# Up-projections of five FFNs, weights stationary and without transposes

## The chip, the cores and the metric

The kernel runs on one core of one Trainium2 chip. The metric is the device time of one execution in microseconds, the median of the runs. The engines are named as in the profile: PE is TensorE (PEld its weight loads), DVE VectorE, ACT ScalarE, POOL GpSimd, SP the queue that issues the DMAs.

## The reference

Two residual blocks over 256 tokens of 1024 channels, in fp32. What the change touches is the feed-forward network, which stands five times in the whole (two in each layer of the first block, one in the second block):

```python
def swiglu(x, w_in, w_out):
    gate, up = jnp.split(x @ w_in, 2, axis=-1)
    return (jax.nn.silu(gate) * up) @ w_out

x = x + 0.5 * swiglu(rms_norm(x, ffn1_norm_g[i]), ffn1_w_in[i], ffn1_w_out[i])
...
def swiglu_2(h, w_gate, w_up, w_down):
    return (jax.nn.silu(h @ w_gate) * (h @ w_up)) @ w_down
```

There are 2816 hidden channels, so `w_in` is 1024 x 5632 (the last FFN has gate and up as two matrices) and `w_out` 2816 x 1024. Between the FFNs stand the mixers: an mLSTM, a sliding-window attention, each with an attention over a memory, and a state-space mixer.

## The kernel before

Every product is made of fp32r parts: a weight is split into `whi` (rounded) and `wlo` (the rest), an activation into hi and lo, and three matmuls, hi x hi, hi x lo and lo x hi, are added up in PSUM.

**Weights.** A chunk is 128 x 1024 weights (512 KB), one step of the inner dimension K for 1024 columns, or two steps for 512. `plan` lists all chunks of the program in the order of use. `load` issues the DMA into one of 5 `raw` buffers, `prepare` (L316) casts `raw` to `whi` on ScalarE (L324) and subtracts on VectorE to make `wlo` (L325, by the helper at L122), each into one of 9 buffers. `need(c)` prepares up to 7 chunks ahead, but no more than 9 beyond the chunks used up.

**Token-major products**, `gemm` (L391): the stationary operand is the activation, 128 tokens by 128 of K, the moving one 512 columns of weights, and the result has tokens on the partitions (L418 hi x hi, L419 hi x lo of the weight, L420 lo x hi). **Channel-major products**, `gemm_ch` (L429), are used in some mixers: the stationary operand is 128 x 128 weights, the moving one the 256 tokens (L440 to L442), and the result has channels on the partitions.

**The FFN.** `ffn_in` takes the hidden channels in six blocks, five of 512 and one of 256. In a block gate and up of both token tiles grow in four PSUM banks (pool `mm`, four banks); ScalarE applies Silu (L563, L569), VectorE multiplies. The down-projection needs the result with channels on the partitions, so `operand_block` has TensorE transpose it (`split_t`, L453, four 128 x 128 to a bank of the other pool), ScalarE copies out the hi part (L455), VectorE the lo part. `residual_gemm` is the down-projection: token-major, the transposed hidden rows stationary (they are called `s` in the profile), added to the residual. `NormT` holds the normed and transposed input of an FFN or mixer, `xh` and `xl`.

**What sets the order.** The kernel is written with a tile library that orders the instructions of each engine by priority and places the waits; each engine then takes its instructions in that order. Transposes and side work are put in between the chunks by `defer`, `later` and `tick`.

Of the kernel before, what the change touches and what calls it, by code (L numbers as in the profile page):

```python
# [10 lines left out]
F32 = mybir.dt.float32  # L11
# [6 lines left out]
P = 128  # L18
# [44 lines left out]
class Operand:  # L63
    """A transposed activation, rows of K on the partitions, as an exact sum hi + lo."""
# [11 lines left out]
class Chunk:  # L76
    """One weight transfer of 1024 elements a partition and the products its columns take part in."""
# [8 lines left out]
def hybrid_kernel(ctx: ExitStack, tc: tile.TileContext, *aps, names=None):  # L86
# [7 lines left out]
    xtp = ctx.enter_context(tc.tile_pool(name="xtp", bufs=4))  # L94
# [46 lines left out]
    # ------------------------------------------------------------ constants  # L141
# [23 lines left out]
    # parameters by channel, transposed once  # L165
# [33 lines left out]
    # rows on every partition  # L199
# [3 lines left out]
    # ------------------------------------------------------------ weights  # L203
# [12 lines left out]
    def spec_ffn_in(w, w_up=None):  # L216
# [13 lines left out]
        blocks = []  # L230
        for b in range(5):
            blocks.append([add(pair(k, 1, 512 * b, 512 * b + 512), [(k, "g", 0, 512), (k, "u", 512, 512)])
                           for k in range(8)])
        blocks.append([add(pair(k, 2, 2560, 2816), [(k + i, "gu", i * 512, 512) for i in range(2)])
# [100 lines left out]
    # Work that the products hide: steps of generators and delayed calls, taken between the chunks.  # L335
# [38 lines left out]
    def pipeline(units, dist):  # L374
        """Starts a unit at each step; a unit goes on to its next stage every dist steps."""
# [15 lines left out]
    def gemm(chunks, xop, evac, groups=None, by_key=False):  # L391
        """Token-major products: evac(tok, key, psum) after each accumulation."""
# [36 lines left out]
    def gemm_ch(chunks, xop, evac):  # L429
        """Channel-major products of 512 columns: evac(pair, psum) with two tiles of 128 channels."""  # L430
# [17 lines left out]
    # ------------------------------------------------------------ activations  # L448
    def split_t(src, nk, dsts):
        """src [tokens, nk*128] transposed, as hi and lo in dsts (APs of [P, nk, 128])."""  # L450
# [15 lines left out]
    def direct_block(op, tok, k0, ps, nk):  # L466
        """An operand from a psum that already holds it transposed."""
# [7 lines left out]
    class NormT:  # L475
        """The normed residual, transposed, for products of either kind."""

        def __init__(self):
            self.filled = set()
            self.hi = [xtp.tile([P, 4, 2, P], F32R, tag="xt", name=nm("xh")) for _ in range(2)]  # L480
            self.lo = [xtp.tile([P, 4, 2, P], F32R, tag="xt", name=nm("xl")) for _ in range(2)]
# [4 lines left out]
        def stat(self, tok, kt):  # L486
            return self.hi[kt // 4][:, kt % 4, tok, :], self.lo[kt // 4][:, kt % 4, tok, :]

# [11 lines left out]
    def inv_rms(sums):  # L500
        """(sums[0] + sums[1] + EPS) ** -0.5 of two columns"""
# [8 lines left out]
    def normed(src, gains, put):  # L510
        """src(j) are the two halves of a row; put(j, normed half)"""
# [20 lines left out]
    def residual_gemm(chunks, xop, scale, after, tail=TAIL):  # L532
        """residual += scale * product; after(tok) when a tile is whole"""
# [15 lines left out]
    def norm_after(row, queue=nc.sync):  # L549
        """An operand to be filled by the gemm before, and the function that fills it."""  # L550
        dst = NormT()
        gains = gain_rows(row, queue)
        return dst, lambda t: norm_residual(t, gains, dst)

    def ffn_in(blocks, xop):
        h = Operand()
        for b, cs in enumerate(blocks):
            keep = {}

            def evac(t, key, ps, b=b, keep=keep):  # L560
                if key == "g":
                    keep[t] = slot()
                    act.activation(out=keep[t], in_=ps, func=AF.Silu)  # L563
                elif key == "u":
                    tt(keep[t], keep[t], ps, ALU.mult)
                    operand_block(h, t, 4 * b, keep[t], 4, D_FFN)
# [830 lines left out]
```

## Time and profile before

| | us |
|---|---|
| median of 3 runs (1619.86 to 1621.65) | 1620.25 |
| span of the profiled execution | 1618.5 |
| PE busy | 1599.2 (99%) |
| PEld busy | 1339.0 (83%) |
| DVE busy | 966.7 (60%) |
| ACT busy | 822.5 (51%) |
| DMA read | 280.34 MB, 174 GB/s over the span |

The profile shows one execution; apart from its span no time of that execution is given. Busy time of PE counts the whole length of a matmul, of which several are under way at once; how long one holds up the next is seen from the starts in the timeline alone. Shares are means over stages that differ.

### The profile page before, as it was taken

How to read it: one execution, taken by the hardware profiler on the slowest of the kernel's cores; microseconds unless marked ns; L12 is line 12 of the kernel's file. 1: busy time of each engine (PE TensorE's matmuls, PEld its weight loads, DVE VectorE, ACT ScalarE, POOL GpSimd, SP SyncE). 2: the span in 40 equal slices, each digit the busy share in tenths (PEclk: the TensorE clock that was granted, in tenths of full speed). 3: DMA queues.
4: the chain of work that ended last, by engine and by line, in shares of the span. 5: the costliest groups of instructions: out<-in, count | busy, mean ns of one | idle time of the engine just before them, and what ended most of it. 6: DMA issues, size and time to landing. Idle time of an engine off the chain costs nothing.

```text
span 1618.5 us, 21426 instructions
## 1 busy us (share of the span) xinstructions
PE 1599.2 (99%) x8124; PEld 1339.0 (83%) x8124; DVE 966.7 (60%) x1372; ACT 822.5 (51%) x1170; POOL 40.7 (3%) x72
## 2 busy tenths in 40 slices
PE   9999999999999999999999999999999999999998
PEld 7888898788888888888788888889899988888886
DVE  6555475558555555546765655368788864575552
ACT  6444365546444444444564544357856553454442
POOL 0000010100000000001100000000000000000000
PEclk9999999999999999999999999999999999999999
DMA  8665374446656566564333766565455566466560
GB/s 271 209 188 196 115 263 144 156 130 211 192 184 196 168 197 187 188 196 164 122 88 108 223 193 195 156 197 184 156 158 145 155 195 182 156 221 188 188 198 27
DMA packets 126971, 282.80 MB, mean 175 GB/s; under 512 B 12286, under 2 KB 23698, under 8 KB 126868
## 3 DMA queue, kind: packets, MB, share of 16 engines
q1 hardware_dynamic: 126868, 281.43, 55.0%
q8 instruction: 64, 1.05, 0.3%
q14 instruction: 39, 0.32, 0.1%
HBM read 280.34 MB, written 1.05 MB: 174 GB/s over the span
## 4 chain that ended last, share of the span: by engine, by line
PE 94%; DVE 2%; issue 1%; ACT 1%; DMA 1%; POOL 1%; SPq 0%; POOLq 0%; ACTq 0%; DVEq 0%
PE ps L418 25%; PE ps L420 25%; PE ps L419 25%; PE ps L440 3%; PE ps L441 3%; PE ps L442 3%; PE ps L453 3%; DMA raw<-in_ffn_w_in_dram 1%; PE ps L625 1%; PE ps L1010 1%; PE ps L1252 1%; POOL t L508 1%; PE ps L1032 1%; DVE wlo L122 1%; ACT whi L324 1%
## 5 line engine op out<-in xcount | busy, mean ns | idle before, releaser
L122 DVE TENSOR_TENSOR wlo<-raw,whi 128x1024 fp32r<-128x1024 f32 (+1 forms) x521 | 628.5, 1213 | 440.3 <-ACT whi L324 433.8
L324 ACT CAST whi<-raw 128x1024 fp32r<-128x1024 f32 (+1 forms) x521 | 543.0, 1044 | 556.4 <-PE ps L420 474.3
L418 PE MATMUL ps<-whi,xh 128*128 128x512 f32 (+2 forms) x1168 | 459.5, 394 | 3.0 <-DVE s L122 1.5
L420 PE MATMUL ps<-whi,xl 128*128 128x512 f32 (+2 forms) x1168 | 451.3, 387 | 0.3 <-DVE xl L122 0.2
L419 PE MATMUL ps<-wlo,xh 128*128 128x512 f32 (+2 forms) x1168 | 450.8, 386 | 0.0
L418 PE MATMUL ps<-whi,s 128*128 128x512 f32 x696 | 278.9, 401 | 0.3 <-ACT s L1329 0.3
L419 PE MATMUL ps<-wlo,s 128*128 128x512 f32 x696 | 274.5, 394 | 0.0
L420 PE MATMUL ps<-whi,s 128*128 128x512 f32 x696 | 274.1, 394 | 0.0
L418 PEld LDWEIGHTS ps<-whi,xh 128*128 128x128 f32 x1168 | 219.7, 188 | 48.1 <-DVE s L122 2.3
L420 PEld LDWEIGHTS ps<-whi,xl 128*128 128x128 f32 x1168 | 219.5, 188 | 45.9 <-DVE xl L122 0.9
L419 PEld LDWEIGHTS ps<-wlo,xh 128*128 128x128 f32 x1168 | 219.9, 188 | 41.5 <-issue 0.3
L420 PEld LDWEIGHTS ps<-whi,s 128*128 128x128 f32 x696 | 130.7, 188 | 30.7
L418 PEld LDWEIGHTS ps<-whi,s 128*128 128x128 f32 x696 | 130.8, 188 | 30.4 <-ACT s L1329 0.8
L419 PEld LDWEIGHTS ps<-wlo,s 128*128 128x128 f32 x696 | 130.9, 188 | 28.7
L440 PE MATMUL ps<-xh,whi 128*128 128x256 f32 x448 | 129.8, 290 | 0.0
L441 PE MATMUL ps<-xl,whi 128*128 128x256 f32 x448 | 127.6, 285 | 0.0
L442 PE MATMUL ps<-xh,wlo 128*128 128x256 f32 x448 | 127.6, 285 | 0.0
L440 PEld LDWEIGHTS ps<-xh,whi 128*128 128x128 f32 x448 | 86.4, 193 | 1.7 <-issue 0.2
L441 PEld LDWEIGHTS ps<-xl,whi 128*128 128x128 f32 x448 | 86.4, 193 | 0.4 <-issue 0.2
L442 PEld LDWEIGHTS ps<-xh,wlo 128*128 128x128 f32 x448 | 86.2, 193 | 0.1
L453 PE MATMUL ps<-ident,s 128*128 128x128 f32 x444 | 66.7, 274 | 2.0 <-DVE s L131 2.0
L453 PEld LDWEIGHTS ps<-ident,s 128*128 128x128 f32 x444 | 54.3, 141 | 16.4 <-issue 1.9
(211 smaller groups left out, 971.8 us busy)
## 6 DMA issues: line engine op xcount, KB each, us to landing
raw<-in_ffn_w_in_dram SPq DMA_DIRECT2D x160, 512.0 KB, 4.7
raw<-in_ffn_w_out_dram SPq DMA_DIRECT2D x88, 512.0 KB, 3.4
raw<-in_w_in_dram SPq DMA_DIRECT2D x80, 512.0 KB, 4.1
raw<-in_a_w_in_dram SPq DMA_DIRECT2D x24, 512.0 KB, 4.6
raw<-in_w_gate_dram SPq DMA_DIRECT2D x44, 256.0 KB, 3.1
raw<-in_w_up_dram SPq DMA_DIRECT2D x44, 256.0 KB
raw<-in_w_down_dram SPq DMA_DIRECT2D x22, 512.0 KB, 3.4
raw<-in_ffn_w_in_dram SPq DMA_DIRECT2D x32, 256.0 KB, 3.3
```

Of the source, the lines that this page charges most:

```text
L122: (eng or dve).tensor_tensor(out=o, in0=a, in1=b, op=op)
L324: act.copy(out=c.hi[:, 0:n], in_=c.raw[:, 0:n])
L418: pe.matmul(out=o, lhsT=xh, rhs=wh, start=first, stop=False)
L419: pe.matmul(out=o, lhsT=xh, rhs=wl, start=False, stop=False)
L420: pe.matmul(out=o, lhsT=xl, rhs=wh, start=False, stop=last)
L440: pe.matmul(out=o, lhsT=wh, rhs=xh, start=kt == 0 and j % 2 == 0, stop=False)
L441: pe.matmul(out=o, lhsT=wh, rhs=xl, start=False, stop=False)
L442: pe.matmul(out=o, lhsT=wl, rhs=xh, start=False, stop=kt == nk - 1 and j % 2 == 1)
L453: pe.transpose(out=ps[:, i * P:(i + 1) * P], in_=src[:, i * P:(i + 1) * P], identity=ident)
L508: pool_e.tensor_tensor(out=o, in0=a, in1=mhalf[:, 0:1].to_broadcast([P, n]), op=ALU.pow)
L625: pe.transpose(out=ps[:, i * P:(i + 1) * P], in_=src[:, i * P:(i + 1) * P], identity=ident)
L1010: pe.matmul(out=s[:, i * w:(i + 1) * w], lhsT=qt[half, (hh // 2) * P:(hh // 2 + 1) * P], rhs=bkt[half, g * SEQ:g * SEQ + w], start=True, s ...
```

## The change

In blocks 1 to 5 of each up-projection the roles are swapped. A half (gate or up of one block) is loaded as four chunks of two K steps by 512 columns, and `gemm_hidden` goes over its four tiles of 128 channels: for each K step the `whi` piece is stationary and meets 512 columns, the hi and the lo of the 256 tokens side by side, and then the `wlo` piece meets the 256 hi columns. The left half of the bank then holds hi x hi + lo x hi, the right half hi x lo, and the evacuation adds the two (ScalarE copies the right half, VectorE adds the left). Gate tiles get a Silu, up tiles a multiplication and a split into hi and lo, which are the operand of the down-projection as they are. `NormT` keeps hi and lo in one tile, so that both can be read as one row of 512. Block 0 stays token-major. The last block, 256 channels, has gate and up in the same four chunks, two tiles of each.

```diff
-    xtp = ctx.enter_context(tc.tile_pool(name="xtp", bufs=4))
+    xtp = ctx.enter_context(tc.tile_pool(name="xtp", bufs=2))
...
-        blocks = []
-        for b in range(5):
-            blocks.append([add(pair(k, 1, 512 * b, 512 * b + 512), [(k, "g", 0, 512), (k, "u", 512, 512)])
-                           for k in range(8)])
-        blocks.append([add(pair(k, 2, 2560, 2816), [(k + i, "gu", i * 512, 512) for i in range(2)])
+        def half(h, k, c0):
+            m = w if w_up is None else (w, w_up)[h]
+            src = m.rearrange("(k p) c -> p k c", p=P)
+            off = h * DFF if w_up is None else 0
+            return [(lambda raw: view(raw, 2, 512), src[:, k:k + 2, off + c0:off + c0 + 512])]
+        blocks = [[add(pair(k, 1, 0, 512), [(k, "g", 0, 512), (k, "u", 512, 512)]) for k in range(8)]]
+        for b in range(1, 5):
+            blocks.append([[add(half(h, k, 512 * b), [(k + i, 0, i * 512, 512) for i in range(2)])
+                            for k in range(0, 8, 2)] for h in range(2)])
+        blocks.append([add(pair(k, 2, 2560, 2816), [(k + i, 0, i * 512, 512) for i in range(2)])
                        for k in range(0, 8, 2)])
...
-            self.hi = [xtp.tile([P, 4, 2, P], F32R, tag="xt", name=nm("xh")) for _ in range(2)]
-            self.lo = [xtp.tile([P, 4, 2, P], F32R, tag="xt", name=nm("xl")) for _ in range(2)]
+            self.x = [xtp.tile([P, 4, 2, 2, P], F32R, tag="xt", name=nm("xt")) for _ in range(2)]
+            self.hi = [x[:, :, 0] for x in self.x]
+            self.lo = [x[:, :, 1] for x in self.x]
...
+        def both(self, kt):
+            return self.x[kt // 4][:, kt % 4].rearrange("p h a b -> p (h a b)")
...
+    def gemm_hidden(chunks, xop, tiles, evac):
+        for i in range(tiles):
+            ps = bank(mm)
+            for c in chunks:
+                if i == 0:
+                    need(c)
+                for kt, _, off, _ in c.entries:
+                    sl = slice(off + i * P, off + (i + 1) * P)
+                    pe.matmul(out=ps, lhsT=c.hi[:, sl], rhs=xop.both(kt), start=kt == 0, stop=False)
+                    pe.matmul(out=ps[:, 0:SEQ], lhsT=c.lo[:, sl], rhs=xop.mov(kt)[0], start=False, stop=kt == 7)
+                if i == tiles - 1:
+                    used[0] += 1
+                if c is chunks[1] or c is chunks[3]:
+                    tick()
+            evac(i, ps)
...
+        def both_parts(dst, ps):
+            act.copy(out=dst, in_=ps[:, SEQ:2 * SEQ])
+            tt(dst, ps[:, 0:SEQ], dst, ALU.add)
+
+        for b in range(1, 6):
+            gate = [slot() for _ in range(2 if b < 5 else 1)]
+            up = [slot() for _ in gate]
+            hi, lo = [[slot(F32R) for _ in gate] for _ in range(2)]
+
+            def gate_evac(i, ps, gate=gate):
+                both_parts(half(gate, i), ps)
+                act.activation(out=half(gate, i), in_=half(gate, i), func=AF.Silu)
+
+            def up_evac(i, ps, b=b, gate=gate, up=up, hi=hi, lo=lo):
+                u, a, z = half(up, i), half(hi, i), half(lo, i)
+                both_parts(u, ps)
+                tt(u, u, half(gate, i), ALU.mult)
+                act.copy(out=a, in_=u)
+                tt(z, u, a.bitcast(F32), ALU.subtract)
+                for t in range(2):
+                    h.parts[t, 4 * b + i] = (a[:, t * P:(t + 1) * P], z[:, t * P:(t + 1) * P])
+            if b < 5:
+                gemm_hidden(blocks[b][0], xop, 4, gate_evac)
+                gemm_hidden(blocks[b][1], xop, 4, up_evac)
+            else:
+                gemm_hidden(blocks[b], xop, 4, lambda i, ps: gate_evac(i, ps) if i < 2 else up_evac(i - 2, ps))
```

The order on TensorE near the start of block 2 of the first FFN, before (`ps` are banks, `s` the product of Silu and up that is transposed, `xh` and `xl` the input):

```order
L418 MATMUL ps_121_609<-whi_89_433,xh_2_113 128x512
L419 MATMUL ps_121_609<-wlo_90_434,xh_2_113 128x512
L420 MATMUL ps_121_609<-whi_89_433,xl_4_115 128x512
L453 MATMUL ps_124_615<-ident_79,s_113_576 128x128 x4
L418 MATMUL ps_118_597<-whi_95_460,xh_2_113 128x512
L419 MATMUL ps_118_597<-wlo_96_461,xh_2_113 128x512
L420 MATMUL ps_118_597<-whi_95_460,xl_4_115 128x512
L418 MATMUL ps_119_601<-whi_95_460,xh_2_113 128x512
L419 MATMUL ps_119_601<-wlo_96_461,xh_2_113 128x512
L420 MATMUL ps_119_601<-whi_95_460,xl_4_115 128x512
L453 MATMUL ps_130_636<-ident_79,s_114_585 128x128 x4
```

And in the same FFN with the change, the first and last pair of block 1's first tile, and the first pair of its second (`xt` holds hi and lo of the input; what is left out repeats the pair by K steps):

```order
L574 MATMUL ps_69_379<-xt_2_113,whi_50_246 128x512
L575 MATMUL ps_69_379<-xt_2_113,wlo_51_247 128x256
...
L574 MATMUL ps_69_379<-xt_3_114,whi_77_394 128x512
L575 MATMUL ps_69_379<-xt_3_114,wlo_78_395 128x256
L574 MATMUL ps_94_447<-xt_2_113,whi_50_246 128x512
L575 MATMUL ps_94_447<-xt_2_113,wlo_51_247 128x256
```

A bank is filled by 16 matmuls in a row and then left, where before four banks took turns by chunks; the transposes of these blocks are gone.

On VectorE, the last up tiles of block 3 with the change (`s_159`, `s_160` are up tiles, `s_157`, `s_158` gate, `s_163`, `s_164` the lo parts; a `wlo` row prepares a chunk of a later half):

```order
L122 TENSOR_TENSOR s_159_873<-ps_194_1030,s_159_873 128x256
L122 TENSOR_TENSOR s_159_873<-s_159_873,s_157_871 128x256
L122 TENSOR_TENSOR s_163_877<-s_159_873,s_161_875 128x256
L122 TENSOR_TENSOR s_160_874<-ps_195_1052,s_160_874 128x256
L122 TENSOR_TENSOR s_160_874<-s_160_874,s_158_872 128x256
L122 TENSOR_TENSOR wlo_208_1109<-raw_182_984,whi_207_1108 128x1024
L122 TENSOR_TENSOR s_164_878<-s_160_874,s_162_876 128x256
L122 TENSOR_TENSOR wlo_211_1116<-raw_185_990,whi_210_1115 128x1024
L122 TENSOR_TENSOR s_160_874<-ps_196_1074,s_160_874 128x256
L122 TENSOR_TENSOR wlo_214_1123<-raw_188_996,whi_213_1122 128x1024
L122 TENSOR_TENSOR s_160_874<-s_160_874,s_158_872 128x256
L122 TENSOR_TENSOR wlo_217_1133<-raw_191_1006,whi_216_1132 128x1024
```

Each up tile has three rows here, add, multiply and subtract, and the four preparations of the next chunks stand among the last two tiles; before, a block had two multiplications and two subtractions of 512 columns.

On VectorE, the end of block 5, from the first up tile (`ps_255`) to the last tile's bank (`ps_256`), with the preparations for the down-projection:

```order
L122 TENSOR_TENSOR s_238_1324<-ps_255_1391,s_238_1324 128x256
L122 TENSOR_TENSOR s_238_1324<-s_238_1324,s_237_1323 128x256
L122 TENSOR_TENSOR wlo_263_1444<-raw_242_1328,whi_262_1443 128x1024
L122 TENSOR_TENSOR s_240_1326<-s_238_1324,s_239_1325 128x256
L122 TENSOR_TENSOR wlo_266_1450<-raw_245_1334,whi_265_1449 128x1024
L122 TENSOR_TENSOR s_238_1324<-ps_256_1413,s_238_1324 128x256
```

The row that reads `ps_256` and so gives its bank back stands behind two `wlo` rows.

## Rows read from the trace of the kernel before

**Rows 1.** The page, part 1: busy us, share of the span, instructions.
```profile
PE 1599.2 (99%) x8124; PEld 1339.0 (83%) x8124; DVE 966.7 (60%) x1372; ACT 822.5 (51%) x1170; POOL 40.7 (3%) x72
```
**Rows 2.** The page, part 4: the chain that ended last, by engine and by line.
```profile
PE 94%; DVE 2%; issue 1%; ACT 1%; DMA 1%; POOL 1%; SPq 0%; POOLq 0%; ACTq 0%; DVEq 0%
PE ps L418 25%; PE ps L420 25%; PE ps L419 25%; PE ps L440 3%; PE ps L441 3%; PE ps L442 3%; PE ps L453 3%; DMA raw<-in_ffn_w_in_dram 1%; PE ps L625 1%; PE ps L1010 1%; PE ps L1252 1%; POOL t L508 1%; PE ps L1032 1%; DVE wlo L122 1%; ACT whi L324 1%
```
**Rows 3.** Windows: the second FFN's up-projection.
```profile
core 0: us, PE busy (x) PEld busy (x) DVE busy (x) ACT busy (x) POOL busy (x), PEclk, DMA share, GB/s
373.41:499.23 125.82, 125.73 (x578) 103.72 (x576) 74.89 (x94) 63.83 (x76) 0.56 (x1) 1.00 0.62 196
```
**Rows 4.** Timeline of PE, first FFN, block 3: start, length in us.
```profile
99.69 0.39 PE L418 MATMUL ps<-whi,xh 128*128 128x512 f32 x1
...
108.99 0.39 PE L420 MATMUL ps<-whi,xl 128*128 128x512 f32 x1
109.22 0.60 PE L453 MATMUL ps<-ident,s 128*128 128x128 f32 x4
109.57 0.48 PE L418 MATMUL ps<-whi,xh 128*128 128x512 f32 x1
109.89 0.39 PE L419 MATMUL ps<-wlo,xh 128*128 128x512 f32 x1
```
**Rows 5.** Timeline of PE, channel-major products of the second block.
```profile
1103.62 0.28 PE L441 MATMUL ps<-xl,whi 128*128 128x256 f32 x1
...
1111.78 0.28 PE L440 MATMUL ps<-xh,whi 128*128 128x256 f32 x1
```
**Rows 6.** Timeline of PE, first mixer: 264 and 256 columns, three of each in turn.
```profile
203.53 0.28 PE L418 MATMUL ps<-whi,xh 128*128 128x264 f32 x1
...
206.04 0.28 PE L418 MATMUL ps<-whi,xh 128*128 128x256 f32 x1
```
**Rows 7.** Timeline of PE, start of the second FFN's down-projection.
```profile
500.85 0.38 PE L453 MATMUL ps<-ident,s 128*128 128x128 f32 x2
500.99 0.48 PE L418 MATMUL ps<-whi,s 128*128 128x512 f32 x1
501.30 0.39 PE L419 MATMUL ps<-wlo,s 128*128 128x512 f32 x1
...
504.32 0.39 PE L420 MATMUL ps<-whi,s 128*128 128x512 f32 x1
```
**Rows 8.** Timeline of PE, from block 0 to block 1 of the first two FFNs.
```profile
60.23 0.39 PE L420 MATMUL ps<-whi,xl 128*128 128x512 f32 x1
60.96 0.50 PE L418 MATMUL ps<-whi,xh 128*128 128x512 f32 x1 [0.33 <-ACT s L563]
...
398.46 0.39 PE L420 MATMUL ps<-whi,xl 128*128 128x512 f32 x1
398.93 0.50 PE L418 MATMUL ps<-whi,xh 128*128 128x512 f32 x1
```
**Rows 9.** Groups by form: busy us, mean ns, idle before and its releasers.
```profile
L122 DVE TENSOR_TENSOR wlo<-raw,whi 128x1024 fp32r<-128x1024 f32 x512 | 622.6, 1223 | 436.9 <-ACT whi L324 430.3 <-DMA raw<-in_w_gate_dram 2.3 <-PE ps L1087 0.7
L324 ACT CAST whi<-raw 128x1024 fp32r<-128x1024 f32 x512 | 537.5, 1052 | 550.1 <-PE ps L420 468.0 <-PE ps L441 50.9 <-DMA raw<-in_ffn_w_in_dram 12.2
L122 DVE TENSOR_TENSOR s<-s,ps 128x256 f32<-128x256 f32 x26 | 10.5, 415 | 2.6 <-ACT s L569 2.5
L569 ACT ACTIVATE s<-ps 128x256 f32<-128x256 f32 x10 | 3.8, 384 | 6.4 <-PE ps L420 6.4
L838 ACT COPY s<-ps 128x256 f32<-128x256 f32 x8 | 2.7, 378 | 1.4 <-DVE t L837 1.4
L122 DVE TENSOR_TENSOR s<-ps,s 128x256 fp32r<-128x256 f32 x10 | 4.2, 417 | 0.0
```
**Rows 10.** Timelines of ACT and DVE, first FFN: one chunk's cast and subtraction.
```profile
101.25 1.05 ACT L324 CAST whi<-raw 128x1024 fp32r<-128x1024 f32 x1 [1.67 <-PE ps L420]
102.34 1.23 DVE L122 TENSOR_TENSOR wlo<-raw,whi 128x1024 fp32r<-128x1024 f32 x1 [1.50 <-ACT whi L324]
```
**Rows 11.** Windows: the edge of blocks 0 and 1, second FFN (columns as rows 3).
```profile
399.00:404.00 5.00, 5.00 (x24) 4.14 (x25) 2.93 (x3) 2.51 (x3) 0.00 (x0) 1.00 0.99 349
```

More of the change, by code (lines that the diff above doesn't have):

```diff
@@ L555, in ffn_in @@
     def ffn_in(blocks, xop):
         h = Operand()
[L557 to L566, printed above, removed]
-                else:
-                    s = slot()
-                    act.activation(out=s[:, 0:256], in_=ps[:, 0:256], func=AF.Silu)
-                    tt(s[:, 0:256], s[:, 0:256], ps[:, 256:512], ALU.mult)
-                    operand_block(h, t, 4 * b, s[:, 0:256], 2)
-            groups = [cs[0:FIRST], cs[FIRST:]] if FIRST < 8 else [cs] if b == 0 else None
-            gemm(cs, xop, evac, groups)
+        keep = {}
@@ new lines, in evac, with half @@
+        def evac(t, key, ps):
+            if key == "g":
+                keep[t] = slot()
+                act.activation(out=keep[t], in_=ps, func=AF.Silu)
+            else:
+                tt(keep[t], keep[t], ps, ALU.mult)
+                operand_block(h, t, 0, keep[t], 4, D_FFN)
+        gemm(blocks[0], xop, evac, [blocks[0][0:FIRST], blocks[0][FIRST:]] if FIRST < 8 else [blocks[0]])
+        def half(s, i):
+            return s[i // 2][:, (i % 2) * SEQ:(i % 2 + 1) * SEQ]
+        def both_parts(dst, ps):
+            act.copy(out=dst, in_=ps[:, SEQ:2 * SEQ])
+            tt(dst, ps[:, 0:SEQ], dst, ALU.add)
@@ new lines, in ffn_in @@
+        for b in range(1, 6):
[16 more added lines that the diff above has]
+                gemm_hidden(blocks[b][1], xop, 4, up_evac)
+            else:
+                gemm_hidden(blocks[b], xop, 4, lambda i, ps: gate_evac(i, ps) if i < 2 else up_evac(i - 2, ps))
```

## The prediction

> **What bounds the kernel now.** I read the page's busy shares first, then the chain that ended last, then the stretches of the FFN up-projections, then TensorE's own timeline, since nothing else can tell what one matmul costs. TensorE is busy 1599.2 of 1618.5 us [rows 1], and the chain runs through it for 94% of the span, three quarters on the three matmul lines of `gemm` [rows 2]. In an up-projection (125.82 us in the second FFN) PE has 125.73 us of work, VectorE 74.9, ScalarE 63.8, at a granted clock of 1.00, which is the 2.4 GHz level [rows 3]. So time moves only if TensorE's stream gets shorter, or if something begins to hold it up.
>
> A busy time is no price here: the 0.39 us of a matmul is longer than the step to the next. In block 3 of the first FFN 42 matmuls of 512 columns start between 99.69 and 109.22: 0.2269 us each; rounding apart, 0.2267 [rows 4]. In the channel-major products of the second block 68 matmuls of 256 columns start between 1103.62 and 1111.78: 0.1200 each [rows 5]. Half the columns save 0.1067 us, so 512 columns are 0.2133 us, and both widths carry the same 0.0133 us on top. The change lives on these two steps.
>
> **Matmuls, the same columns in more pieces.** Blocks 1 to 5 of an FFN are 18 tiles of 128 channels for gate and 18 for up. A tile is 8 pairs of one 512-wide and one 256-wide matmul: 8 x (0.2267 + 0.1200) = 2.774 us. Token-major, the same columns were 12 matmuls of 512. So a tile gains 4 instructions: 36 x 4 x 5 FFNs = 720, at 0.0133 us each **+9.6 us**. Bounds: nothing if the 256-wide one hides its part; above, see the first rival. I take 0.0133 because rows 5 have the new roles exactly (weights stationary, `xh` moving), and because alternating widths carry no surcharge: 21 matmuls of 264 and 256 columns in turn step 0.1195 on average [rows 6].
>
> The Trainium skill, "TensorE: Matmul & The Clock Gate", section "Back-to-back issue gap", gives N/2.4 + 2.5 ns for a lone matmul at the higher clock. By it the 720 would cost 1.8 us. The rows differ from it at both widths.
>
> **Transposes.** Of the 44 transposes of an FFN's hidden rows 36 go: eight groups of four and two groups of two. Four of them start at 109.22 and the second matmul behind starts at 109.89; 0.67 less one normal step is 0.443 us [rows 4], which also pays for the slower first matmul behind them. Two cost 1.30 - 0.85 - 0.227 = 0.223 [rows 7]. So 40 x 0.443 + 10 x 0.223 = **-19.9 us**. Bounds: the groups stand on the path, so no more than this; 40 x 0.35 + 10 x 0.14 = 15.4 if the slow first matmul came from something else and stayed.
>
> **Block edges.** Before, all four `mm` banks of a block finish within its last chunk, and the next block wants them at once. At the first edge of the first FFN a step is 0.73 instead of 0.23, in the second 0.47 [rows 8]: 0.5 and 0.24, and the other three are no longer than that; I put 1.2 us for the five. A tile now owns one bank and meets it again four tiles on, so these go: **-1.2** (0 to -2). At the other end comes something new: the down-projection wants the last tile's bank 9 or 10 matmuls (2.0 to 2.3 us) after that tile's end, and in the order on VectorE two `wlo` subtractions stand ahead of its release. Worked out from the end of the tile before: ScalarE copy to 0.38, first `whi` cast from 0.69, where TensorE frees its buffer (two pairs into the last tile), to 1.75, `hi` cast to 2.13, second `whi` cast to 3.18, copy of the last tile to 3.56; VectorE `wlo` 1.8 to 3.0, lo to 3.4, `wlo` to 4.7, the release at 5.1, wanted at 4.8 to 5.0. About 0.2 us each time: **+1.0** (0 to 2).
>
> **Evacuation, costed at nothing.** A gate tile now takes copy, add, Silu; an up tile copy, add, multiply, cast, subtract, all 128x256. Per block that is 16 pieces on each engine, at 0.415 on VectorE and 0.38 on ScalarE, plus 8 weight preparations at 1.223 and 1.052 [rows 9]: VectorE 16.4, ScalarE 14.5 of the 22.19 us that TensorE needs for 8 tiles. What covers it is three other banks: a tile's bank is wanted 3 x 2.77 = 8.3 us after its end. The order on the two engines puts no more than two preparations between a tile's copy and its release. Cast and subtraction of one chunk hand over in 0.04 us (101.25 + 1.05 to 102.34) [rows 10]. If the cover were gone, see the second rival.
>
> **Loads.** Buffers of a half (4 chunks) now come free within its last tile, so four preparations fall close together, and so do the four loads that their `raw` buffers release. DMA moved 349 GB/s at the first block edge [rows 11], 1.5 us a chunk, and has a half, 11.1 us, for four: no price. SP issues 32 DMAs fewer, since gate and up of the last FFN come in one transfer a chunk instead of two; the gains of the next norm still stand among the loads of the down-projection. Block 0, the down-projections and the mixers keep their order.
>
> **Sum.** -19.9 + 9.6 - 1.2 + 1.0 = -10.5 us. The profiled execution has a span of 1618.5; no other time is shown for it, and the median of the runs, 1620.25, stands 1.75 above. With the same 1.75 around a span of 1608.0 the forecast is **1609.8 us**. An up-projection like the second should go from 125.82 to 124.0 (8 x 0.443 gone, 1.92 and no edge).
>
> **Rivals.**
> *The 512-wide stream doesn't settle.* In the down-projection the very same 512-wide matmuls step 13 times in 3.02 us: 0.2323, not 0.2267 [rows 7]; in the up-projection a dozen steps behind a transpose are as slow. Something in the stream decides, and no row has 512 and 256 in turn. If all 1440 wide matmuls pay it: 1440 x 0.0056 = 8.1 us, giving 1617.9. For it: the alternation is new. Against: rows 5 and 6 are settled with these roles and with mixed widths. 18%.
> *Evacuation holds TensorE* (the slower side). ScalarE and VectorE wait for each other four times an up tile, and preparations stand in the same queues. In a row without overlap an up tile takes 0.417 + 0.415 + 0.378 + 0.417 and three handovers of 0.04, 1.75 us (its copy beside the last subtraction), a gate tile 1.3, a preparation 2.3: 4 x 1.75 + 4 x 1.3 + 8 x 2.3 = 30.6 a block against 22.2. Half of that overrun, 4.2 us in 4.5 blocks, less the 8.3 us that the banks lend, is 10.6 us an FFN: 53 us, 1663. It decides from 2.3 us a block on ((8.3 + 2.1) / 4.5, with 2.1 what an FFN gains), that is with two thirds of the preparations' time uncovered. Against: the sums above and the order, in which casts run while VectorE works. The Trainium skill's main page, "Trainium Kernel Development and Optimization", section "Best Practices", warns that tiling for TensorE doesn't speed up PSUM evacuation; that is this rival, and the trace of before can't show it. 10%.
> *The pieces are free*: the 0.0133 us of a 256-wide matmul hide behind the wide one before it. Then 9.6 drops out: 1600.2. Against it, rows 6, where the shorter of two widths pays it in full. 6%. By the page's 2.5 ns, cited above, it would be 1602.0.
> That the transposes stay is excluded by the order.
>
> **Numbers.** Forecast 66%, own range 1605 to 1613 (the edges' bounds, and part of the other bounds of the first two terms). The range holds it and most of the first rival: 1605 to 1618.5. A measurement here can tell about 0.2%, 3.2 us, so no change is 1617.0 to 1623.5. Faster: 66 + 6 + a third of the first rival, 6 = 78%. Same: the rest of that rival, 12%. Slower: 10%.
>
> **What would show it.** TensorE's timeline in a hidden tile: starts 0.227 and 0.120 apart, a tile every 2.77 us, no bracketed idle at the two `gemm_hidden` lines; 264 transposes of `split_t` instead of 444; up-projections of 124 us. 0.232 behind the wide ones speaks for the first rival; idle before a tile's first matmul released by VectorE's add for the second, and released by a `wlo` or a DMA it would be the loads, which I left out. VectorE's busy time should rise by 75 to 108 us: 360 new pieces of 0.416, 150 us, against 80 of 512 and 20 of 256 columns that go (42 us if a wide one cost no more than a narrow one, 75 if twice as much); ScalarE's by 69 to 99. Both without effect.

## The result, and the profile after

The changed kernel takes 1605.95 us (median of 4 runs, 1604.94 to 1608.11) against 1620.08 for the kernel before on the same chip (1619.86 to 1621.65): a ratio of 0.9914, interval 0.9902 to 0.9926. The forecast was 1609.8 in 1605.0 to 1618.5. The profiled execution has a span of 1603.2 us instead of 1618.5, 15.3 less, where the steps of the prediction add up to 10.5.

The page after, parts 1 and 4 (against [rows 1, 2]):

```profile
PE 1583.9 (99%) x8664; PEld 1355.3 (85%) x8664; DVE 1037.7 (65%) x1632; ACT 886.1 (55%) x1430; POOL 39.7 (2%) x72
...
PE 93%; DVE 2%; issue 1%; DMA 1%; ACT 1%; POOL 1%; SPq 0%; POOLq 0%; DVEq 0%; ACTq 0%
```

The groups of PE after, by line (count | busy us, mean ns | idle just before them):

```profile
L574 PE MATMUL ps<-xt,whi 128*128 128x512 f32 x1440 | 500.6, 392 | 0.0
L575 PE MATMUL ps<-xt,wlo 128*128 128x256 f32 x1440 | 403.2, 280 | 0.0
...
L458 PE MATMUL ps<-ident,s 128*128 128x128 f32 x264 | 38.4, 273 | 0.8 <-DVE s L131 0.8
```

TensorE is still the bound at 99%, with 540 records more and 15 us less of busy time. The hidden tiles are two lines of 1440 matmuls with no idle time in front of them: evacuation holds nothing up. 264 transposes of `split_t` are left of 444.

To see where the time went I cut both executions at the same places. Windows of the kernel before: first FFN, first mixer, second and third FFN, fourth FFN, fifth FFN, and then of the second FFN alone blocks 1 to 5 and the down-projection (columns in the first line):

```profile
core 0: us, PE busy (x) PEld busy (x) DVE busy (x) ACT busy (x) POOL busy (x), PEclk, DMA share, GB/s
11.77:203.53 191.76, 190.91 (x858) 155.86 (x859) 106.41 (x116) 92.18 (x112) 1.10 (x2) 0.99 0.60 193
203.53:373.41 169.88, 165.45 (x907) 140.82 (x906) 107.32 (x183) 93.72 (x158) 10.13 (x17) 0.99 0.54 172
373.41:750.17 376.76, 376.68 (x1706) 308.73 (x1704) 207.75 (x230) 175.95 (x209) 2.20 (x4) 1.00 0.59 187
...
873.76:1062.09 188.33, 188.33 (x853) 154.37 (x852) 103.15 (x107) 87.82 (x104) 1.11 (x2) 1.00 0.60 187
...
1424.43:1611.48 187.05, 187.05 (x845) 153.50 (x843) 94.80 (x99) 79.73 (x97) 1.10 (x2) 1.00 0.51 166
396.65:499.23 102.58, 102.50 (x470) 84.53 (x468) 56.58 (x56) 48.41 (x56) 0.00 (x0) 1.00 0.64 199
499.23:561.86 62.63, 62.63 (x277) 50.66 (x276) 30.30 (x32) 25.98 (x31) 0.55 (x1) 1.00 0.54 170
```

The same stretches of the kernel after:

```profile
11.79:200.17 188.38, 187.04 (x967) 158.64 (x967) 119.55 (x167) 104.61 (x164) 1.11 (x2) 1.00 0.61 195
200.17:368.54 168.37, 163.92 (x908) 139.45 (x907) 106.96 (x182) 94.15 (x158) 9.14 (x17) 1.00 0.54 175
368.54:739.77 371.23, 371.23 (x1921) 315.95 (x1920) 236.56 (x333) 201.07 (x313) 2.21 (x4) 1.00 0.59 190
...
863.46:1049.20 185.74, 185.74 (x962) 157.98 (x961) 116.78 (x158) 100.50 (x156) 1.11 (x2) 1.00 0.58 190
...
1411.43:1596.21 184.78, 184.78 (x953) 156.98 (x951) 109.14 (x151) 92.89 (x149) 1.10 (x2) 1.00 0.51 168
391.74:492.10 100.36, 100.36 (x582) 88.48 (x580) 68.26 (x105) 59.65 (x108) 0.00 (x0) 1.00 0.60 196
492.10:554.10 62.00, 62.00 (x274) 50.32 (x273) 32.97 (x35) 26.66 (x32) 0.55 (x1) 1.00 0.57 179
```

Read down the first number: -3.38, -1.51, -5.53 (two FFNs), -2.59, -2.27; the other two mixers differ by 0.1 each way. So 13.8 us lie in the five FFNs, and **1.5 us in a mixer whose instructions the change leaves alone**. In the second FFN, blocks 1 to 5 give 2.22 and the down-projection 0.63.

The new tiles can be read off the timeline of PE after, second FFN, around the one group of transposes that block 0 still sends into block 1:

```profile
395.61 0.40 PE L574 MATMUL ps<-xt,whi 128*128 128x512 f32 x1
395.85 0.28 PE L575 MATMUL ps<-xt,wlo 128*128 128x256 f32 x1
395.97 0.60 PE L458 MATMUL ps<-ident,s 128*128 128x128 f32 x4
396.33 0.48 PE L574 MATMUL ps<-xt,whi 128*128 128x512 f32 x1
396.65 0.28 PE L575 MATMUL ps<-xt,wlo 128*128 128x256 f32 x1
396.77 0.39 PE L574 MATMUL ps<-xt,whi 128*128 128x512 f32 x1
397.00 0.28 PE L575 MATMUL ps<-xt,wlo 128*128 128x256 f32 x1
397.11 0.39 PE L574 MATMUL ps<-xt,whi 128*128 128x512 f32 x1
```

A pair (396.77 to 397.11) steps 0.347 us, 0.230 for the wide matmul and 0.117 for the narrow one; forecast were 0.2267 + 0.1200, which is the same sum. The group costs what two pairs take beyond 0.693: 396.77 - 395.61 = 1.16, so 0.46.

### The profile page after: what moved, and what is told of

It is laid out like the page before. It is cut to its first block, busy times and chain, and to the rows that moved or that the text cites. A ratio compares the mean times of both kernels' runs of the same rounds, so it can differ in the third digit from the quotient of the medians.

```text
span 1603.2 us, 22953 instructions
## 1 busy us (share of the span) xinstructions
PE 1583.9 (99%) x8664; PEld 1355.3 (85%) x8664; DVE 1037.7 (65%) x1632; ACT 886.1 (55%) x1430; POOL 39.7 (2%) x72
## 4 chain that ended last, share of the span: by engine, by line
PE 93%; DVE 2%; issue 1%; DMA 1%; ACT 1%; POOL 1%; SPq 0%; POOLq 0%; DVEq 0%; ACTq 0%
PE ps L574 20%; PE ps L423 15%; PE ps L425 15%; PE ps L424 15%; PE ps L575 11%; PE ps L445 3%; PE ps L446 3%; PE ps L447 3%; PE ps L458 2%; PE ps L1061 1%; PE ps L1303 1%; PE ps L676 1%; POOL t L517 1%; DVE wlo L122 1%; PE ps L1083 1%
## 5 line engine op out<-in xcount | busy, mean ns | idle before, releaser
L574 PE MATMUL ps<-xt,whi 128*128 128x512 f32 x1440 | 500.6, 392 | 0.0
L575 PE MATMUL ps<-xt,wlo 128*128 128x256 f32 x1440 | 403.2, 280 | 0.0
L574 PEld LDWEIGHTS ps<-xt,whi 128*128 128x128 f32 x1440 | 269.4, 187 | 59.1
L575 PEld LDWEIGHTS ps<-xt,wlo 128*128 128x128 f32 x1440 | 272.2, 189 | 0.2
L122 DVE TENSOR_TENSOR s<-ps,s 128x256 f32<-128x256 f32 (+1 forms) x218 | 101.3, 468 | 120.3 <-ACT s L600 100.8
L423 PE MATMUL ps<-whi,xt 128*128 128x512 f32 (+2 forms) x448 | 174.2, 389 | 3.2 <-ACT xt L460 1.8
L425 PE MATMUL ps<-whi,xt 128*128 128x512 f32 (+2 forms) x448 | 170.1, 381 | 1.2 <-DVE xt L122 1.2
L424 PE MATMUL ps<-wlo,xt 128*128 128x512 f32 (+2 forms) x448 | 169.8, 379 | 0.0
L445 PE MATMUL ps<-xt,whi 128*128 128x256 f32 x448 | 129.1, 288 | 0.0
L122 DVE TENSOR_TENSOR s<-s,s 128x256 f32<-128x256 f32 (+2 forms) x228 | 107.7, 478 | 32.5 <-ACT s L616 18.0
L446 PE MATMUL ps<-xt,whi 128*128 128x256 f32 x448 | 127.0, 284 | 0.0
L447 PE MATMUL ps<-xt,wlo 128*128 128x256 f32 x448 | 126.8, 284 | 0.0
L600 ACT COPY s<-ps 128x256 f32<-128x256 f32 x180 | 66.2, 368 | 86.7 <-PE ps L575 84.8
L423 PEld LDWEIGHTS ps<-whi,xt 128*128 128x128 f32 x448 | 84.4, 188 | 19.9 <-ACT xt L460 2.2
```

The source lines that it names most:

```text
L122: (eng or dve).tensor_tensor(out=o, in0=a, in1=b, op=op)
L423: pe.matmul(out=o, lhsT=xh, rhs=wh, start=first, stop=False)
L424: pe.matmul(out=o, lhsT=xh, rhs=wl, start=False, stop=False)
L425: pe.matmul(out=o, lhsT=xl, rhs=wh, start=False, stop=last)
L445: pe.matmul(out=o, lhsT=wh, rhs=xh, start=kt == 0 and j % 2 == 0, stop=False)
L446: pe.matmul(out=o, lhsT=wh, rhs=xl, start=False, stop=False)
```

## Where the 15.3 us are

For blocks 1 to 5 of the second FFN the arithmetic closes. Before: 432 matmuls at 0.2267 are 97.92; of 102.58 remain 4.66, of them 0.25 at the edge [rows 8] and 4.41 for nine groups of transposes, **0.49 a group**. Read directly it is a little less: blocks 2 to 4 start 22.70 to 22.72 us apart, with 96 matmuls (21.76) and two groups in each, 0.47 to 0.48 a group. The difference is slower steps behind the edge, so the split between groups and edges is good to about 1 us over five FFNs. After: 288 pairs at 0.34667 are 99.84; the other 0.52 of 100.36 are the one group that stays and twelve slower pairs ahead of it. Over five FFNs these stretches sum to 512.98 before and 502.01 after, -10.97: +9.6 for the matmuls, -19.6 for 40 groups, -1.0 for edges. The down-projections give -2.14, block 0 -0.68 (0.57 of it in the first FFN, where loads still come in), the first mixer -1.51.

**The first mixer** is the part that does not belong to the change. Windows in the two executions, behind a wait of TensorE for VectorE (1.98 us before, 1.76 after):

```profile
226.50:230.50 4.00, 4.00 (x24) 4.00 (x23) 3.17 (x10) 3.22 (x4) 0.00 (x0) 0.57 0.94 273
```
```profile
222.90:226.50 3.60, 3.60 (x32) 3.60 (x31) 2.94 (x10) 3.22 (x5) 0.00 (x0) 1.00 0.92 283
```

Before, the granted clock behind the wait was 0.57 for this window (the 1.2 GHz level for most of it: 15 matmuls of 256 columns step 0.213 us instead of 0.120), after, 1.00. Both stretches lie in the same product, right behind the wait. That is worth 1.4 us, and it could be the length of the wait or chance. The first two runs look at that.

## The experiments

**The same two kernels again.** No edit to either.

> The changed kernel once more, unaltered. If the 1.5 us that the first mixer gave belong to one execution (TensorE waits there for VectorE, 1.98 us before and 1.76 us after, and only before did 16 steps of 256 columns behind it take 0.213 instead of 0.120 us), some executions here will have the slow steps too and lie 1.5 us above the fastest; if they belong to the change, none has. Ratio to before 0.9905 to 0.992, span 1603 to 1605.

> The kernel before once more, for a second trace of it. If the slow steps in the first mixer come with the length of the wait ahead of them, they are there again, with a wait of about 2 us; if they are chance, they may be missing, with a span of about 1617.0. The FFN stages should repeat within 0.1 us: second up-projection 125.8, its down-projection 62.3.

Measured: the changed kernel 1604.78 us (1604.27 to 1605.99), ratio 0.9905 (0.9889 to 0.9922), span 1602.6; the five hidden stretches repeat (100.58, then 100.36 three times, 100.35). The kernel before 1620.42 (one run), span 1618.7. Its windows, the start of the first FFN and the first mixer without its edges:

```profile
11.50:39.09 27.59, 26.82 (x112) 21.64 (x113) 21.10 (x23) 18.03 (x23) 0.56 (x1) 0.88 0.78 255
204.90:246.00 41.10, 38.79 (x317) 37.60 (x316) 31.98 (x65) 26.21 (x40) 4.11 (x4) 1.00 0.76 262
```

In this execution of the same kernel the mixer has the full clock, and the lower clock stands longer in the first FFN's block 0 (27.59 us at 0.88, where the first execution took 26.14 at 0.93). So where the clock falls can differ between two executions of one kernel. The wait in the mixer, in the first execution and in this one:

```profile
225.63 0.44 PE L625 MATMUL ps<-ident,s 128*128 128x128 f32 x2 [1.98 <-DVE s L122]
```
```profile
227.14 0.44 PE L625 MATMUL ps<-ident,s 128*128 128x128 f32 x2 [1.91 <-DVE s L122]
```

It is 0.07 us shorter where the clock stayed up. In the fourteen profiled executions of this case the clock fell behind the longest wait of this stage in the five where that wait was longest (1.98 to 2.44 us: the kernel before, the transposes put back, the wide form in the mixers, the other places in SBUF, the later query transposes) and stayed at 1.00 in the nine others (1.16 to 1.91 us). So it is hardly mere chance: it went with the length of the wait, which differs between executions. In the changed kernel the wait was 1.76 and 1.16 us; whether the change itself shortens it is not shown. Without these two places the change gives about 13.2 us of the 15.3 (15.27 less 1.51 and 0.57); the medians of the two series differ by 14.1 and 15.8 (the kernel before beside the second: 1620.54, eight runs).

**The price of a matmul.** The wide one is cut in two:

```diff
-  pe.matmul(out=ps, lhsT=c.hi[:, sl], rhs=xop.both(kt), start=kt == 0, stop=False)
+  pe.matmul(out=ps[:, 0:SEQ], lhsT=c.hi[:, sl], rhs=xop.mov(kt)[0], start=kt == 0, stop=False)
+  pe.matmul(out=ps[:, SEQ:2 * SEQ], lhsT=c.hi[:, sl], rhs=xop.mov(kt)[1], start=False, stop=False)
```

> In the hidden tiles the 512-wide matmul is cut in two of 256, same columns, same banks, same evacuation: 1440 more matmuls. If every matmul carries a fixed 0.0133 us, a tile goes from 2.774 to 2.88 us and the kernel gains 1440 x 0.0133 = 19.2 us on the changed one: about 1625, slower than before. If a fixed price is only paid between unlike widths or after a wide one, the three 256-wide steps would be 0.107 to 0.117 each and the time 1590 to 1612.

Measured: 1626.65 us, ratio 1.0032 (1.0019 to 1.0045): the gain is gone and a little more. The window of the second FFN's hidden stretch, 100.36 in the changed kernel:

```profile
397.01:501.12 104.11, 104.11 (x870) 104.10 (x868) 68.28 (x105) 60.06 (x107) 0.00 (x0) 1.00 0.59 189
```

3.75 us for 288 matmuls more, 0.0130 each; all five stretches together 18.7 us for 1440. The term of +9.6 stands. The rival that the pieces are free falls. By the gap that the Trainium skill gives for an isolated matmul ("TensorE: Matmul & The Clock Gate", section "Back-to-back issue gap", 2.5 ns) the cut would have cost an estimated 3.6 us; the 18.7 measured decide against it for this stream, in which every matmul loads weights of its own.

**The price of a transpose.** Nine groups per FFN go back into TensorE's queue, and nothing reads them:

```diff
+            def dummy(n):
+                pd = bank()
+                for k in range(n):
+                    pe.transpose(out=pd[:, k * P:(k + 1) * P], in_=ident, identity=ident)
...
+                if i % 2 == 1:
+                    defer(4, lambda: dummy(4))
```

> The changed kernel with nine groups of four transposes per FFN put back into TensorE's queue, of a constant, read by nobody. If the transposes' own time on TensorE was the gain, 45 groups at 0.46 us (the price of the one group that the changed kernel still has in each FFN's block 1: steps of 0.718 and 0.437 where 0.347 twice is normal) give back 20.8 us: about 1626.5. If the gain came from what surrounded them (copies and subtractions, banks, waits), these add under 10 us: below 1616.

Measured: 1630.04 us, ratio 1.0058 (1.0043 to 1.0073). The span is 25.7 longer than that of the repeated changed kernel: 21.3 in the hidden stretches, 2.2 in the down-projections, and 2.3 in the first mixer, where this execution has the low clock. 23.5 us for 45 groups are 0.52 each, more than expected. The gain was the transposes' own time on TensorE. Why 0.52 and not 0.46 shows in the steps: after some groups the pairs go on at 0.353 instead of 0.347 us until the next group (below).

**The cover of the evacuation.** Two banks, then one, for the four tiles of a half:

```diff
+        banks = [bank(mm), bank(mm)]
         for i in range(tiles):
-            ps = bank(mm)
+            ps = banks[i % 2]
```

> Within a half the four hidden tiles use two banks in turn, so a tile's bank is wanted again one tile (2.77 us) after its end instead of three. In the changed kernel a bank is read out 1.03 to 2.66 us after its tile's end (mean 1.55). By that nothing waits, or a few tenths of a us a block: 1605 to 1610. If evacuation were close to the limit with three spare banks (the second rival), TensorE would now wait in most tiles: over 1625.

> One bank for the four tiles of a half: three of four tiles wait for the read-out of the one before. At the shortest read-out, 1.03 us, 27 waits an FFN are 139 us; at the lags of the changed kernel (8.58 us a block) 193: 1745 to 1800. If fewer, the matmuls that follow a wait hide part of it.

Two banks: 1614.28 us, ratio 0.9971 (0.996 to 0.9983), slower than the 1605 to 1610 expected. The hidden stretches grow by 1.2 to 1.5 us each, yet no wait is listed at their lines. The timeline of PE there, second FFN, shows one small hitch and what follows it, and the timeline of VectorE the addition that reads the bank out:

```profile
422.21 0.39 PE L575 MATMUL ps<-xt,whi 128*128 128x512 f32 x1
...
422.90 0.39 PE L575 MATMUL ps<-xt,whi 128*128 128x512 f32 x1
423.13 0.28 PE L576 MATMUL ps<-xt,wlo 128*128 128x256 f32 x1
423.27 0.47 PE L575 MATMUL ps<-xt,whi 128*128 128x512 f32 x1
...
423.69 0.40 PE L575 MATMUL ps<-xt,whi 128*128 128x512 f32 x1
...
424.41 0.40 PE L575 MATMUL ps<-xt,whi 128*128 128x512 f32 x1
```
```profile
422.71 0.41 DVE L122 TENSOR_TENSOR s<-ps,s 128x256 f32<-128x256 f32 x1
```

Two pairs take 0.69 us up to 422.90 and 0.72 from 423.69 on. The hitch between them (0.79 from 422.90 to 423.69) is 0.1 us, where a tile begins (423.27) and wants the bank back that VectorE has read until 423.12, 2.65 us after its tile's end. From there the mean pair is 0.3533 us, to the end of the stretch. So with one spare bank evacuation still costs only 0.1 us of waits in this FFN; the rest is the matmul stream, which left one rhythm for another.

One bank: 1712.69 us, one run, below the expected 1745 to 1800. Windows of the second FFN, from the first hidden tile to the last, and the rest of the down-projection:

```profile
414.66:544.64 129.98, 118.37 (x619) 94.79 (x618) 68.19 (x106) 60.14 (x108) 0.00 (x0) 1.00 0.46 152
544.64:598.10 53.46, 53.46 (x236) 43.17 (x235) 32.06 (x33) 26.03 (x31) 0.55 (x1) 1.00 0.64 209
```

The hidden stretch is 29.6 us longer for 27 waits, 1.1 each, close to the shortest read-out of 1.03. But 37 of the down-projection's matmuls run inside it (619 records where the changed kernel has 582), since the library put them into the waits, and the down-projection is 8.5 shorter. Evacuation without cover costs about 21 us an FFN; with three spare banks, nothing.

**Block 0 channel-major as well.** `blocks[0]` is loaded and computed as the others, and `gemm_hidden` waits for both token tiles:

```diff
-        for b in range(1, 6):
+        for b in range(6):
...
+                    until(lambda: xop.has(0, kt) and xop.has(1, kt))
```

> Block 0 is channel-major too. On TensorE's own account that saves 10 groups of transposes (0.46 to 0.52 us, 4.6 to 5.2) and costs 160 matmuls at 0.0133 (2.1): 2.5 to 3.1 us faster. But a channel-major tile wants all 256 tokens: the second half of the normed input comes 8 us after the last matmul ahead of the FFN (the sums from 368.9 to 370.2, Square to 371.7, the power on POOL to 373.3, the scaling to 374.7, transposes and copies to about 376.7, with the last matmul at 368.3), which block 0 hid by doing the first token tile. Five such waits are 40 us, and a fall of the clock behind them may add 1.5 each: 1640 to 1655. If the norm is not what block 0 was left for, 1603.

Measured: 1654.19 us, ratio 1.0215 (1.019 to 1.0241). Windows ahead of the second FFN's first tile and behind it:

```profile
377.00:386.10 9.10, 3.33 (x15) 2.37 (x13) 8.27 (x20) 4.57 (x8) 0.56 (x1) 0.82 0.87 312
386.10:390.00 3.90, 3.84 (x13) 3.31 (x14) 2.35 (x13) 1.77 (x4) 0.00 (x0) 0.55 0.01 4
```

TensorE works 3.33 of 9.10 us while the norm of the last tokens goes through VectorE, and then starts at a granted clock of 0.55. From the last matmul ahead of the second to fifth FFN to its down-projection 132.1 to 134.2 us pass, 123.8 in the changed kernel. Token-major block 0 is what hides the norm; the 2.5 us that its transposes would give are not to be had this way.

**The wide form in the mixers.** `gemm_ch` calls `gemm_hidden`, and a copy and an addition bring each tile to a slot before its old evacuation:

```diff
...
+            act.copy(out=dst, in_=ps[:, SEQ:2 * SEQ])
+            tt(dst, ps[:, 0:SEQ], dst, ALU.add)
+            if i % 2 == 1:
+                evac(i // 2, s[0])
+        gemm_hidden(chunks, xop, 4, whole)
```

> The channel-major products of the mixers (14 products of 4 tiles, three 256-wide matmuls a K step) take the hidden tiles' form, 512 and 256: 448 matmuls fewer, 448 x 0.0133 = 6.0 us on TensorE. Each tile adds a copy on ScalarE and an addition on VectorE (56 each, 0.37 and 0.42 us, 23 us of VectorE, which is 60 to 88% busy in the second block). If TensorE is the only bound there: 1599. If VectorE's queue holds products up: same or slower than 1605.

Measured: 1623.18 us, ratio 1.0016 (1.0006 to 1.0026): the gain is lost. Windows of the third mixer here, and in the repeated changed kernel:

```profile
1057.04:1427.28 370.24, 361.19 (x1862) 300.24 (x1861) 273.30 (x447) 231.96 (x372) 10.34 (x10) 1.00 0.53 167
```
```profile
1048.53:1410.78 362.25, 361.88 (x2246) 320.60 (x2245) 258.35 (x400) 214.27 (x320) 8.11 (x10) 1.00 0.56 170
```

384 records fewer, and 8 us longer: PE idles 9.05 us instead of 0.37. Of that 4.7 us, in two waits (the longer 4.1), stand in front of the wide matmul of `gemm_hidden`, and both are ended by an addition that reads a bank out; the rest stands at other lines of the mixer that wait for VectorE or ScalarE. Here VectorE has its own long chains, and the same evacuation that is free in an FFN holds TensorE. Another 3.7 us are two of the five hidden stretches at 102.2, in code that this edit leaves alone; 3.1 lie in the first mixer, where the clock fell behind a wait of 2.44 us, and 3.2 ahead of block 1 of the first FFN, which this edit leaves alone too.

**What decides the rhythm?** The same 1.8 us jumps had come up in two runs, so three more look at it. First the place in SBUF, by the order of three pool lines (`sp` ahead of `wpool`):

> Only the places in SBUF change: the slots (whose hi and lo parts are stationary in the down-projection) lie ahead of the weights instead of behind. In every run so far 512-wide token-major steps with a slot stationary take 0.232 us and with the normed input stationary 0.227. If the place decides, the down-projections (264 steps, 62.0 us) fall to about 60.5, 1.5 us each, and the other products with slots stationary (768 steps) by 4 us: 1605 to 1594; or the up-projections rise instead. If the stream's own order decides, nothing moves beyond 2 us.

Measured: 1612.45 us, ratio 0.9945 (0.9929 to 0.9962). Neither forecast came as written. The down-projections don't move (61.2 to 62.0 us from the first start to the last; 61.0 to 62.0 in the changed kernel), so the theory of the place falls. But the hidden stretches of the third and fifth FFN are 102.20 and 102.17, the others 100.3 to 100.8, together 3.9 us more than in the changed kernel; the rest of the difference lies in the first block 0 and the first mixer. Then the place of the one group of transposes, by one step each way:

```diff
-D_FFN = 4
+D_FFN = 5
```

> The changed kernel with the transposes of block 0's hidden rows one step later (in block 1 behind 16 pairs instead of 12). In the runs so far the pairs of a hidden stretch step either 0.3467 us for hundreds of pairs, or 0.3533 in a pattern of three (0.350, 0.361, 0.349), and change only where something interrupts the stream: the group of transposes or a wait. If each interruption draws the pattern anew, some of the five stretches (36 tiles, 100.36 us in the fast pattern) come out near 102.2: each 1.8 us, 1605 to 1614 in all. If the pattern belongs to the tiles' own order, all five stay at 100.4 and the time at 1605.

> The same with the transposes one step earlier (behind 8 pairs). By the same theories: five stretches of 100.3 and 1605 if the order decides, some of 102.2 (1.8 us each, up to 1614) if each interruption draws anew.

Measured: 1613.05 us later (ratio 0.9953, 0.9937 to 0.9968) and 1612.48 earlier (0.995, 0.993 to 0.9969), 6.5 to 8.3 us slower than the two medians of the changed kernel, with the same instructions. The hidden stretches hold 7.4 us of that in the first and 3.8 in the second, whose first block 0 and mixer took 2.4 us more. Windows of the first three hidden stretches, one step later:

```profile
37.61:138.22 100.61, 100.61 (x584) 88.70 (x583) 68.82 (x110) 62.23 (x110) 0.00 (x0) 1.00 0.62 198
391.71:493.90 102.19, 102.19 (x581) 88.73 (x580) 68.36 (x105) 60.05 (x107) 0.00 (x0) 1.00 0.59 194
579.10:681.29 102.19, 102.19 (x582) 88.64 (x580) 68.25 (x105) 60.00 (x107) 0.00 (x0) 1.00 0.58 193
```

Four of five stretches are slow here, two of five with the group one step earlier, none in the changed kernel. In every stretch the pairs run at 0.350, 0.361, 0.349 in turn up to the group; behind it they either go on so, or fall into 0.347, 0.347, 0.346 and stay there. So a rhythm changes only where something interrupts the stream, a group or a wait. It is not drawn anew in each execution: the repeat of the changed kernel has the same five fast stretches. Nor is the group's place all that decides: with the other places in SBUF, and with the wide form in the mixers, two of five stretches were slow although the group stands where it does in the changed kernel. What decides was not found.

**The wait in the first mixer.** Its query transposes come two steps later:

```diff
-        defer(D_HEAD, go)
+        defer(D_HEAD + 2 if layer == 0 else D_HEAD, go)
```

> The changed kernel with the query transposes of the first mixer two steps later (7 instead of 5), so that VectorE's result is there when TensorE comes to them. In the changed kernel TensorE waits 1.76 us for it, and in some executions runs 16 or so steps at the lower clock behind it (1.5 us). If the wait is the cause of both, this stage falls by about 1.8 us, no execution has slow steps there, and the time is 1601.5 to 1603.5; the five hidden stretches stay at 100.4. If VectorE is only late because of what stands ahead of it, the wait moves with the transposes or to the next consumer, and nothing is gained.

Measured: 1607.0 us (1606.19 to 1609.35), ratio 0.9922 (0.9908 to 0.9936), no gain. The timeline of PE in that stage:

```profile
234.39 0.39 PE L810 MATMUL ps<-t,tri 128*128 128x4 f32 x2 [2.08 <-DVE t L122]
```

The wait moved to the next consumer of VectorE's results and is longer, and in this execution the low clock (0.58 from 235.4 to 239.5) follows it there. The second theory holds. None of the versions tried beats the changed kernel.

## Why the prediction was right

**The bound** was read rightly: TensorE's own stream set the time, and the term for the matmuls, worked out from its steps, came within 0.5 us; the other two were off by 1 to 2 us each.

**Matmuls, +9.6:** confirmed by the pair step of 0.3467 and by cutting the wide ones (0.0130 for 0.0133). That 0.2267 and 0.1200 come out as 0.230 and 0.117 changes nothing in the sum.

**Transposes, -19.9:** the mechanism was right and the size a little low. I took the step with the group and the next one, 0.443; a group costs 0.47 to 0.49, because five to eight steps behind the slow one are still unsettled (about 0.231 us instead of 0.2267). My upper bound ("no more than this") was wrong for that reason: by 0.49, 40 groups are 19.6 and not 17.7, 1.9 more.

**Block edges, -1.2 and +1.0:** the old edges were 1.0 (0.50, 0.25, 0.15, 0.14 and nothing). The 0.73 that I took for the first edge of the first FFN stands between blocks 1 and 2: block 1 begins at 37.91 us and block 2 at 60.96. (In the same way the 42 matmuls of [rows 4] run on into block 4, which begins at 106.50; the step read from them stands.) The new term failed: nothing waits. Timelines of VectorE and PE after, start of the second down-projection:

```profile
492.71 1.22 DVE L122 TENSOR_TENSOR wlo<-raw,whi 128x1024 fp32r<-128x1024 f32 x1
493.84 0.42 DVE L122 TENSOR_TENSOR s<-ps,s 128x256 f32<-128x256 f32 x1
```
```profile
493.95 0.40 PE L425 MATMUL ps<-whi,s 128*128 128x512 f32 x1
494.19 0.63 PE L423 MATMUL ps<-whi,s 128*128 128x512 f32 x2
```

The release comes at 493.84 + 0.42 = 494.26, 0.2 us earlier than I worked out. The matmul that wants the bank is the second of the two in the last row, at about 494.42: the first belongs to the next chunk and another bank, since the library had put it ahead. The bank is wanted at the 11th matmul and not at the 9th or 10th. So +1.0 should have been 0, with 0.16 us to spare, and so in all five FFNs.

**Evacuation at nothing** was right, and the two-bank run shows by how much: in the changed kernel a bank is read out 1.0 to 2.7 us after its tile's end in all but one tile (3.2), and wanted after 8.3. VectorE's busy time rose by 71.0 us and ScalarE's by 63.6, both just under the forecast (75 to 108, 69 to 99). Neighbouring pieces overlap, as in the VectorE rows above (493.84 is before 492.71 + 1.22), and busy time counts that once; the lengths of all pieces, added up, rise by 88.6 and 84.8, as forecast.

**Rivals.** *Evacuation holds TensorE* did not come in the FFNs; its mechanism is what made the third mixer slower in the wide form. The warning of the Trainium skill's main page ("Trainium Kernel Development and Optimization", "Best Practices") holds there, with 4.7 us of idle in front of the wide matmuls, and not in the FFNs, with 0.0. *Pieces free* fell. *The 512-wide stream doesn't settle* did not come in this kernel, but it was more real than 18% says: the slow rhythm exists, costs 1.83 us a stretch, 9 us over five (I had 8.1), and came in two or four of five stretches in four runs that leave the matmuls of these tiles as they are: one group of transposes earlier or later, other places in SBUF, other products in the mixers. That all five stretches were fast in the changed kernel, in both of its profiled executions, followed from nothing that I had worked out: here the forecast's likeliest case came true by luck.

**What stood in no step:** 1.5 us in the first mixer and 0.6 in the first block 0, where the lower clock falls in some executions and not in others. They and the two mis-sized terms make the 4.8 us between -10.5 and -15.3: 1.9 (groups), 0.9 (the down-projections gave 2.1, where 10 groups of two and the new edge were to give 1.2), 1.5 (mixer) and 0.7 (block 0), less 0.2 for the old edges. The range held it only just: 1605.95 is 0.95 above its lower end, and the repeat, 1604.78, 0.2 below it.

## What to carry to other kernels

Price a matmul by the step to the next start, split it into columns and a fixed part with rows of two widths, and price an interruption over all the steps until the rhythm is back, not over the first two. Extra evacuation is free only as far as spare banks cover the read-out, so compare the lag of the read-out with the time until the bank is wanted, stage by stage: the same form was free in an FFN and a loss in a mixer. Repeat the old kernel's profile before crediting a change with a stage that it doesn't touch.

## What the runs showed of the hardware that I had not expected

- A stream of alternating 512- and 256-wide matmuls showed two stable rhythms at a granted clock of 1.00: 0.3467 us a pair, or 0.3533 in a cycle of three. It holds one for hundreds of matmuls, and the changed kernel's two profiled executions had the same one in the same stretches. What decides is open. Streams of 256 alone, in the cut version, had only one: 0.1200.
- 512-wide token-major steps take 0.232 us with a slot as stationary operand and 0.227 to 0.228 with the normed input, in every stage of every run read for it, and also with the slots elsewhere in SBUF. Why is open.
- Behind the same wait of TensorE in the first mixer the clock fell to 1.2 GHz in one execution of the kernel before (wait of 1.98 us, 1.4 us lost) and not in another (1.91 us). Over all fourteen profiled executions it fell there in the five with the longest waits, 1.98 to 2.44 us, and in none of the nine with 1.16 to 1.91.
